# Low parts at three stage heads: subtracted by VectorE instead of GpSimd

## The chip, the cores and the metric

The kernel runs on one core of a Trainium2 chip. The metric is device time in microseconds (us), from the first to the last instruction and what lies around them, of one execution of the whole program. Engines are called as in the profile: PE (matrix products) with PEld (its weight loads), DVE (VectorE), ACT (ScalarE), POOL (GpSimd), SP (SyncE, which here only starts transfers).

## What is computed

A decoder trunk of two layers on 256 tokens of width 1024, in float32. Each layer has a token mixer and a channel mixer, and after each of the four the sum with the input is normalised.

```python
x = layernorm(ALPHA * x + mixer_ab(x))      # gated linear attention | top-k sparse attention
x = layernorm(ALPHA * x + swiglu(x))        # dense, 1024 -> 2816 -> 1024
x = layernorm(ALPHA * x + mixer_cd(x))      # forgetting attention | dilated attention
x = layernorm(ALPHA * x + moe(x))           # the best 2 of 8 experts, 1024 -> 3584 -> 1024
def swiglu(x, w1, w3, w2): return (silu(x @ w1) * (x @ w3)) @ w2
```

The router takes x @ w_router, keeps the two best experts of a token and weighs their outputs by a softmax of the two values.

## The kernel before, in words

**Products in three parts.** Every large product is made in a shorter float format of PE (float32r), with each operand split in a high part (the value cast to float32r) and a low part (value minus high part). `mm3` (lines 190 to 195) sums high x high, low x high and high x low in one PSUM bank. So each weight has to be split on its way from memory to PE, and so has each activation.

**Weights.** `piece` (from line 142) loads one piece of a weight, mostly 1 MB, in a raw buffer of a ring (`raw`), and splits it in two or four cuts: ACT casts the high part `whi` (line 165), and another engine subtracts it to get the low part `wlo` (line 167). There are six buffers of each, and the ring has 5 raw buffers at first and 13 at the end. The transfers are started on SP (line 152) and wait there, in order, until a raw buffer is free, that is until its last subtraction is done. Normally the subtraction is DVE's. A counter, `pool_lo`, gives the next one, two or three pieces to POOL instead:

```python
        eng = nc.vector
        if self.pool_lo > 0:
            self.pool_lo -= 1
            eng = nc.gpsimd
```

It is set to 2 ahead of the first pieces of the dense network (line 710) and of the second mixer (line 738), and to 1 ahead of the experts (line 955). The pieces there are, for the dense network, the two halves of the first 512 columns of w1 (four cuts of 1024 columns); for the second mixer, a piece of 264 columns (four cuts of 528) and one of 256 columns (two cuts of 1024); for the experts the first half of the first expert's w1 (two cuts of 1024).

**A stage's head.** A stage ends with a residual norm in two token tiles of 128 tokens. For each tile DVE adds the product to x (line 258, two steps), makes the mean (274), subtracts it and multiplies by the gain (279, two steps), makes the variance (281); ACT squares (276) and POOL takes the reciprocal root (282); DVE finishes x (285, two steps). Then PE transposes x (238), ACT casts the high part xTh (187) and DVE subtracts the low part xTl (188), each in two halves per tile. The first products of the next stage need xTh, xTl, whi and wlo. They are made for the first token tile while the second is still in its norm.

**The experts' head.** `begin`, in `moe_fast`, is written out by hand for PE, ACT, DVE and POOL. The router's values of a tile go through lines 845 to 848 (`best_two`), then a cast of the indices to float (857), a compare (859) and a sum to `sel` (861). PE counts the tokens in front (865, 866), DVE makes `slot` (867) and one-hot matrices `G` (908), and PE gathers the tokens of an expert by products of G with the high parts `xh` and the low parts `xl` of x (913). ACT and DVE take the results out of PSUM (919, 921). The split of x in xh and xl is line 964 (ACT) and 965 (POOL).

**Order.** Outside the hand-written part, a scheduler that simulates the program sets the order of the instructions of each engine. Each engine works in that order and waits at its instruction until the operands are there.

Of the kernel before, what the change touches and what calls it, by code (L numbers as in the profile page):

```python
# [9 lines left out]
F32 = mybir.dt.float32  # L10
# [66 lines left out]
def drain(*gens):  # L77
    for g in gens:
        for _ in g:
            pass  # L80
# [23 lines left out]
def lead(n, k):  # L104

    return [(t, i) for i in range(n - k) for t in range(NT)] + [(t, i) for t in range(NT) for i in range(n - k, n)]


class Trunk:
    def __init__(self, ctx, tc, io):  # L110
        self.ctx, self.tc, self.nc, self.io = ctx, tc, tc.nc, io
        self.pool_lo = 0
        pool = lambda name, bufs, **kw: ctx.enter_context(tc.tile_pool(name=name, bufs=bufs, **kw))
        self.cst = pool("cst", 1)
        self.raw = pool("raw", 5)
        self.rings, self.turn = [self.raw] * 5, 0
        self.hip = pool("hip", 6)
        self.lop = pool("lop", 6)
        self.dram = pool("dram", 1, space=DRAM)
        self.junk = dict(tag="X", bufs=2)  # L120
        self.ps = pool("ps", 4, space=PSUM)
        self.pa = pool("pa", 4, space=PSUM)
# [19 lines left out]
    def piece(self, src, later=False, cuts=2, raw=None):  # L142

        nc = self.nc
        srcs = src if isinstance(src, list) else [src]
        n, w = srcs[0].shape[1], sum(s.shape[2] for s in srcs)
        raw = (self.ring(n * w) if raw is None else raw).rearrange("p (n w) -> p n w", n=n)
        c = 0  # L150
        for s in srcs:
            nc.sync.dma_start(raw[:, :, c:c + s.shape[2]], s)
            c += s.shape[2]
        eng = nc.vector
        if self.pool_lo > 0:
            self.pool_lo -= 1
            eng = nc.gpsimd
        h = n // cuts
        parts = {}

        def split(i):
            sl = slice(i * h, (i + 1) * h)
            hi = self.hip.tile([128, h, w], F32R, name="whi", tag="whi")
            lo = self.lop.tile([128, h, w], F32R, name="wlo", tag="wlo")
            nc.scalar.copy(hi, raw[:, sl])  # L165
            parts[i] = hi, lo
            return lambda: eng.tensor_sub(lo, raw[:, sl], hi.bitcast(F32))  # L167

        part = lambda j, c0, c1: [a[:, j % h, c0:c1] for a in parts[j // h]]
        if later:  # L170
            return part, split
        for i in range(cuts):
            split(i)()
        return part
# [509 lines left out]
    def ffn(self, x):  # L684
        nc, io = self.nc, self.io
        with ExitStack() as st:
            pool = lambda n, b: st.enter_context(self.tc.tile_pool(name=n, bufs=b))
            acts, early = pool("acts", 2), pool("early", 1)
            self.wk, m = pool("wk1", 1), pool("m1", 1)
            xT = self.pair(early, [128, KT, S], "xT")  # L690
            gT = [m.tile([128, DFF // 128, S], F32R, name=n) for n in ("gTh", "gTl")]
            for c0 in range(0, DFF, 512):
                wd = min(512, DFF - c0)
                act = acts.tile([128, NT, 512], F32, name="act")

                def e1(t, p):
                    nc.scalar.activation(act[:, t, :wd], p, AF.Silu)

                def e3(t, p):
                    nc.vector.tensor_mul(act[:, t, :wd], act[:, t, :wd], p)  # L700
                    q = self.abank()
                    for j in range(wd // 128):
                        nc.tensor.transpose(q[:, j * 128:(j + 1) * 128], act[:, t, j * 128:(j + 1) * 128],
                                            self.ident)
                    sl = (slice(None), slice(c0 // 128, (c0 + wd) // 128), slice(t * 128, (t + 1) * 128))
                    self.split(gT[0][sl], gT[1][sl], q[:, :wd].rearrange("p (a b) -> p a b", b=128))

                first = self.proj_n(io["w1_dense"], c0, wd, xT, e1)
                if c0 == 0:
                    self.pool_lo = 2  # L710
                    self.transposed(xT, x, 0)
                    drain(islice(first, 2))
                    self.transposed(xT, x, 1)
                drain(first, self.proj_n(io["w3_dense"], c0, wd, xT, e3))
            drain(self.out_proj(io["w2_dense"], lambda k: [a[:, k] for a in gT], lead(DFF // 256, 3), x, 0, 1))


    def mixer_cd(self, x, scr, spare):
        nc, io = self.nc, self.io
        w = io["w_in_cd"]  # L720
        with ExitStack() as st:
# [13 lines left out]
                nc.scalar.copy(vc[:, t, 256:512], p[:, 0:256])  # L735
                nc.vector.tensor_copy(fz[:, t], p[:, 256:264])

            self.pool_lo = 2
            self.turn = 5
            first = [self.proj_n(w, 1280, 264, xT, evac_f), self.proj_n(w, 1024, 256, xT, self.evac_n(vc))]  # L740
            for t in range(NT):
# [158 lines left out]
    def moe_fast(self, x):  # L900

        nc, io, f, late = self.nc, self.io, self.f, self.late
# [3 lines left out]
        def one_hot(G, e, t):  # L906
            for a in range(2):
                nc.vector.tensor_scalar(G[:, t, a], self.iota[:, 1:129], self.slot[:, t, e + a:e + a + 1],
                                        None, op0=OP.is_equal)

        def collect(p, G, i, k, t):
            for j in range(2):
                nc.tensor.matmul(p[:, j * 256:(j + 1) * 256], self.xhl[i][:, t, (k + j) * 128:(k + j + 1) * 128],
                                 G[:, t], start=(t == 0 and j == 0), stop=(t == 1), skip_group_check=True)
# [8 lines left out]
        def xg_tiles():  # L923
            return [[self.xg.tile([128, KT, 128], F32R, name=n, bufs=2) for n in ("xgh", "xgl")] for a in range(2)]
# [24 lines left out]
        def begin():  # L949

            xh, xl = self.xhl
            E = mybir.EngineType
            G = f.tile([128, NT, 2, 128], F32R, name="G")
            xg = xg_tiles()
            self.pool_lo = 1
            part, split = [], []
            for w, k0 in (("w1_moe", 0), ("w1_moe", 4), ("w3_moe", 0)):
                p, sp = self.piece(self.rows(io[w][0], k0, 4, 0, 512), later=True)
                part.append(p)
                split.append(sp)  # L960
            ph = [self.abank() for _ in range(KT // 2)]

            def parts(t):
                nc.scalar.copy(xh[:, t], x[:, t])
                nc.gpsimd.tensor_sub(xl[:, t], x[:, t], xh[:, t].bitcast(F32))

            with self.tc.manual_schedule(engines={E.PE, E.Activation, E.DVE, E.Pool}):
                pos = self.bank()
                parts(0)
                with self.tc.issue_after(self.squares.ins):  # L970
                    lo = [split[0](0), split[0](1)]
                with self.tc.issue_after(self.power.ins):
                    for l in lo:
                        l()
                self.logits(1)
                best = self.route(f, pos)
                parts(1)
                lo = [split[1](0), split[1](1)]
                for t in range(NT):
                    one_hot(G, 0, t)  # L980
                for k in range(0, KT, 2):
                    for t in range(NT):
                        collect(ph[k // 2], G, 0, k, t)
                for l in lo:
                    l()
                for a in range(2):
                    for k in range(0, KT, 2):
                        evacuate(xg, ph[k // 2], 0, k, a)
                for l in (split[2](0), split[2](1)):
                    l()  # L990
                self.combine_weights(*best)
            for k in range(0, KT, 2):
                p = self.abank()
                for t in range(NT):
                    collect(p, G, 1, k, t)
                for a in range(2):
                    evacuate(xg, p, 1, k, a)
            transposed_one_hot(G, 0, xg)
            q = self.abank()
            for t in range(NT):  # L1000
                nc.tensor.matmul(q[:, 0:8], self.ones, self.sel[:, t], start=(t == 0), stop=(t == 1))
            mx = f.tile([128, 1], F32, name="mx")
            nc.vector.tensor_reduce(mx, q[:, 0:8], axis=AX.X, op=OP.max)
            nc.vector.tensor_copy(self.mxi, mx)
            return part
# [59 lines left out]

        SP = (0, 2, True, 0)
        ahead = begin()
        prev = None
        for e, c in product(range(NE), range(NC)):
# [18 lines left out]
            if (e, c) == (0, 3):  # L1088
                x = self.xp.tile([128, NT, D], F32, name="sum", tag="x")
# [139 lines left out]
```

## Time and profile before

| | us |
|---|---|
| median of three runs | 1510.81 (1510.8 to 1512.51) |
| the profiled execution, its time | 1513.67 |
| its span, first to last instruction | 1511.8 |
| PE busy in the span | 1462.5 (97%) |
| DVE busy | 1201.2 (79%) |
| ACT busy | 1025.9 (68%) |
| POOL busy | 91.2 (6%) |
| `wlo` subtractions on DVE (799) | 953.8, mean 1.229 each |

The mean granted clock of PE is 0.981 of full speed. The stages lie in the span as follows: first mixer up to about 168 us, dense network to 363, second mixer to 497, experts to the end. A row of a timeline gives the start, the duration (of the whole group if several alike follow each other), the engine, the line, the operation, what it writes and reads, the shape, the count, and in brackets how long the engine stood idle ahead of it and what ended that. Matrix instructions overlap, so the distance between the starts of two tells more than their durations.

### The profile page before, as it was taken

Reading aid. Unit: us, or ns where it says so; the run is one execution under the profiler, and the core shown is the slowest. Engines: PE = TensorE matmul, PEld = TensorE weight load, DVE = VectorE, ACT = ScalarE, POOL = GpSimd, SP = SyncE. Lnnn points to the kernel's source line nnn. Section 1 sums busy time; section 2 is a strip of 40 time slices with the busy share of each in tenths; the row PEclk is TensorE's granted clock in tenths of the full one; section 3 lists DMA queues with packets and bytes.
Section 4 is the critical chain, followed back from the end, with each engine's and each line's share of the span. In section 5 each row is a group of like instructions: output and inputs, shape, how many; then the busy total and the mean of one; then the engine's idle time right before and its main releaser. Section 6 shows DMA issues by size and latency. Waiting matters only on the chain. (4 is left out here: it accounts for less than half of the span.)

```text
span 1511.8 us, 19538 instructions
## 1 busy us (share of the span) xinstructions
PE 1462.5 (97%) x7226; PEld 1208.5 (80%) x7226; DVE 1201.2 (79%) x1394; ACT 1025.9 (68%) x1328; POOL 91.2 (6%) x85
## 2 busy tenths in 40 slices
PE   6999899998999799999999999999999999999996
PEld 5987688887987688888888888888888887888885
DVE  3697464545555899999999999989889889889987
ACT  3647444433676678878878878887777677777764
POOL 2223300003100230000000000000000000000000
PEclk8999999999999899999999999999999999999998
DMA  8844465556546689999989999999999999999971
GB/s 218 256 139 130 169 232 194 176 187 197 179 121 242 206 298 388 392 355 367 373 319 370 371 363 362 375 327 351 374 335 354 359 358 324 378 358 359 364 259 57
DMA packets 199459, 435.99 MB, mean 288 GB/s; under 512 B 9298, under 2 KB 33658, under 8 KB 199360
## 3 DMA queue, kind: packets, MB, share of 16 engines
q1 hardware_dynamic: 195760, 429.88, 79.7%
q10 hardware_dynamic: 2848, 2.95, 1.1%
q0 software_dynamic: 752, 1.88, 0.5%
q8 instruction: 58, 0.95, 0.3%
q14 instruction: 41, 0.34, 0.1%
HBM read 432.77 MB, written 1.84 MB: 287 GB/s over the span
## 5 line engine op out<-in xcount | busy, mean ns | idle before, releaser
L167 DVE TENSOR_TENSOR wlo<-raw,whi 128x1024 fp32r<-128x1024 f32 (+1 forms) x799 | 953.8, 1229 | 157.7 <-ACT whi L165 137.5
L165 ACT CAST whi<-raw 128x1024 fp32r<-128x1024 f32 (+1 forms) x811 | 821.1, 1046 | 209.8 <-PE bank L195 133.0
L193 PE MATMUL bank<-whi,xgh 128*128 128x512 f32 x896 | 353.9, 396 | 0.0
L194 PE MATMUL bank<-wlo,xgh 128*128 128x512 f32 x896 | 352.4, 393 | 0.0
L195 PE MATMUL bank<-whi,xgl 128*128 128x512 f32 x896 | 351.0, 392 | 0.1
L194 PEld LDWEIGHTS bank<-wlo,xgh 128*128 128x128 f32 x896 | 168.5, 188 | 40.5 <-DVE wlo L167 4.8
L195 PEld LDWEIGHTS bank<-whi,xgl 128*128 128x128 f32 x896 | 168.3, 188 | 36.7 <-ACT xgl L919 0.4
L193 PEld LDWEIGHTS bank<-whi,xgh 128*128 128x128 f32 x896 | 168.5, 188 | 35.6
L194 PE MATMUL y<-wlo,gTh 128*128 128x512 f32 x440 | 173.5, 394 | 0.0
L195 PE MATMUL y<-whi,gTl 128*128 128x512 f32 x440 | 171.6, 392 | 0.7 <-DVE gTl L188 0.7
L193 PE MATMUL y<-whi,gTh 128*128 128x512 f32 x440 | 149.3, 392 | 0.0
L195 PE MATMUL bank<-whi,xTl 128*128 128x512 f32 (+2 forms) x288 | 108.3, 377 | 9.7 <-DVE xTl L188 9.7
L193 PE MATMUL bank<-whi,xTh 128*128 128x512 f32 (+2 forms) x288 | 107.8, 375 | 2.6 <-ACT xTh L187 2.6
L194 PE MATMUL bank<-wlo,xTh 128*128 128x512 f32 (+2 forms) x288 | 107.5, 374 | 0.0
L195 PEld LDWEIGHTS y<-whi,gTl 128*128 128x128 f32 x440 | 82.6, 188 | 18.4 <-DVE gTl L188 1.2
L194 PEld LDWEIGHTS y<-wlo,gTh 128*128 128x128 f32 x440 | 82.7, 188 | 17.8 <-DVE wlo L167 0.3
L193 PEld LDWEIGHTS y<-whi,gTh 128*128 128x128 f32 x440 | 82.6, 188 | 17.8
L187 ACT CAST gTh<-abank 128x512 fp32r<-128x512 f32 (+1 forms) x67 | 38.8, 579 | 73.8 <-PE y L194 53.8
L193 PE MATMUL bank<-xTh,whi 128*128 128x256 f32 (+1 forms) x264 | 78.9, 299 | 7.6 <-ACT whi L165 7.6
L282 POOL TENSOR_TENSOR lnst<-lnst,mhalf 128x1 f32<-128x1 f32 x8 | 4.9, 613 | 1235.3 <-DVE lnst L281 1235.3
L195 PE MATMUL bank<-xTh,wlo 128*128 128x256 f32 (+1 forms) x264 | 78.5, 300 | 0.7 <-DVE wlo L167 0.7
L194 PE MATMUL bank<-xTl,whi 128*128 128x256 f32 (+1 forms) x264 | 78.5, 298 | 0.0
(293 smaller groups left out, 1478.4 us busy)
## 6 DMA issues: line engine op xcount, KB each, us to landing
raw<-in_w_moe SPq DMA_DIRECT2D x333, 1024.0 KB, 6.7
raw<-in_w_dense SPq DMA_DIRECT2D x33, 1024.0 KB, 5.1
raw<-in_w_in_ab SPq DMA_DIRECT2D x13, 1024.0 KB, 11.8
raw<-in_w_in_cd SPq DMA_DIRECT2D x11, 1024.0 KB, 5.9
raw<-in_w_out_ab SPq DMA_DIRECT2D x4, 1024.0 KB, 5.0
raw<-in_w_out_cd SPq DMA_DIRECT2D x4, 1024.0 KB, 5.8
T<-scr_bias ACTq DMA_DIRECT2D x8, 256.0 KB, 5.4
raw<-in_w_moe SPq DMA_DIRECT2D x3, 512.0 KB, 4.2
```

What stands on the lines that cost most here:

```text
L165: nc.scalar.copy(hi, raw[:, sl])
L167: return lambda: eng.tensor_sub(lo, raw[:, sl], hi.bitcast(F32))
L187: self.nc.scalar.copy(hi, src)
L193: mm(out, a[0], b[0], start=start, stop=False, skip_group_check=True)
L194: mm(out, a[0], b[1], start=False, stop=False, skip_group_check=True)
L195: return mm(out, a[1], b[0], start=False, stop=stop, skip_group_check=True)
L282: self.power = nc.gpsimd.tensor_tensor(st[:, 5:6], st[:, 4:5], self.mhalf[:, 0:1], op=OP.pow)
```

## The change

The counter is gone, and with it POOL's subtractions: all of them are DVE's. In the experts' head, where the order is written by hand, the subtractions also move: they come behind the one-hot matrices and the gather of the high parts, the first weight subtraction first, then the two of x, then the other weight subtractions.

```diff
@@ piece @@
-        eng = nc.vector
-        if self.pool_lo > 0:
-            self.pool_lo -= 1
-            eng = nc.gpsimd
...
-            return lambda: eng.tensor_sub(lo, raw[:, sl], hi.bitcast(F32))
+            return lambda: nc.vector.tensor_sub(lo, raw[:, sl], hi.bitcast(F32))
@@ ffn, mixer_cd, begin @@
-                    self.pool_lo = 2
-            self.pool_lo = 2
-            self.pool_lo = 1
@@ begin @@
-            def parts(t):
-                nc.scalar.copy(xh[:, t], x[:, t])
-                nc.gpsimd.tensor_sub(xl[:, t], x[:, t], xh[:, t].bitcast(F32))
+            def low(t):
+                nc.vector.tensor_sub(xl[:, t], x[:, t], xh[:, t].bitcast(F32))
...
-                parts(0)
+                nc.scalar.copy(xh[:, 0], x[:, 0])
                 with self.tc.issue_after(self.squares.ins):
                     lo = [split[0](0), split[0](1)]
-                with self.tc.issue_after(self.power.ins):
-                    for l in lo:
-                        l()
                 self.logits(1)
                 best = self.route(f, pos)
-                parts(1)
-                lo = [split[1](0), split[1](1)]
+                nc.scalar.copy(xh[:, 1], x[:, 1])
+                lo += [split[1](0), split[1](1)]
...
-                for l in lo:
+                lo[0]()
+                low(0)
+                low(1)
+                for l in lo[1:]:
                     l()
```

Line numbers of the changed kernel are 5 to 9 lower from `piece` on (line 167 is 162 there, 188 is 183, 258 is 253, 274 is 269, 279 is 274, 908 is 901). POOL loses fourteen rows and DVE gains them; no instruction of PE, ACT or SP is added or taken away.

On DVE at the dense network's head (lnst are the norm's sums, lngb its gain and bias), from the second token tile's residual on, before:

```order
L258 SCALAR_TENSOR_TENSOR xcur,lnst<-xcur,bank 128x512 x2
L167 TENSOR_TENSOR wlo<-raw,whi 128x1024
L274 TENSOR_SCALAR lnst<-lnst 128x1
L167 TENSOR_TENSOR wlo<-raw,whi 128x1024
L188 TENSOR_TENSOR xTl<-abank,xTh 128x4x128
```

and now:

```order
L162 TENSOR_TENSOR wlo<-raw,whi 128x1024 x3
L253 SCALAR_TENSOR_TENSOR xcur,lnst<-xcur,bank 128x512
L162 TENSOR_TENSOR wlo<-raw,whi 128x1024
L253 SCALAR_TENSOR_TENSOR xcur,lnst<-xcur,bank 128x512
L162 TENSOR_TENSOR wlo<-raw,whi 128x1024 x2
L183 TENSOR_TENSOR xTl<-abank,xTh 128x4x128 x2
```

Six subtractions stand ahead of xTl where two stood, and the mean (line 274, now 269) has moved behind xTl.

On DVE at the second mixer's head, from the first token tile's variance on, before:

```order
L281 TENSOR_SCALAR lnst<-lnst 128x1
L285 SCALAR_TENSOR_TENSOR xcur<-bank,lnst,lngb 128x512 x2
L258 SCALAR_TENSOR_TENSOR xcur,lnst<-xcur,bank 128x512 x2
L274 TENSOR_SCALAR lnst<-lnst 128x1
L279 SCALAR_TENSOR_TENSOR bank<-xcur,lnst,lngb 128x512 x2
L188 TENSOR_TENSOR xTl<-abank,xTh 128x4x128 x2
```

and now:

```order
L162 TENSOR_TENSOR wlo<-raw,whi 128x528
L280 SCALAR_TENSOR_TENSOR xcur<-bank,lnst,lngb 128x512 x2
L162 TENSOR_TENSOR wlo<-raw,whi 128x528 x3
L253 SCALAR_TENSOR_TENSOR xcur,lnst<-xcur,bank 128x512 x2
L162 TENSOR_TENSOR wlo<-raw,whi 128x1024
L269 TENSOR_SCALAR lnst<-lnst 128x1
L162 TENSOR_TENSOR wlo<-raw,whi 128x1024
L183 TENSOR_TENSOR xTl<-abank,xTh 128x4x128
L274 SCALAR_TENSOR_TENSOR bank<-xcur,lnst,lngb 128x512 x2
L183 TENSOR_TENSOR xTl<-abank,xTh 128x4x128
```

The six subtractions are there now, and the first half of xTl has moved ahead of the two steps of line 279 (now 274).

On DVE at the experts' head, from the one-hot matrices G on, before:

```order
L908 TENSOR_SCALAR G<-iota,slot 128x128 x4
L167 TENSOR_TENSOR wlo<-raw,whi 128x1024 x4
L875 TENSOR_TENSOR f_4483<-comb 128x2
L921 CAST xgl<-abank 128x256 x4
```

and now:

```order
L901 TENSOR_SCALAR G<-iota,slot 128x128 x4
L162 TENSOR_TENSOR wlo<-raw,whi 128x1024
L956 TENSOR_TENSOR xl<-xcur,xh 128x1024 x2
L162 TENSOR_TENSOR wlo<-raw,whi 128x1024 x5
L868 TENSOR_TENSOR f_4480<-comb 128x2
L914 CAST xgl<-abank 128x256 x4
```

Two subtractions of x and two of weights have come in; all that stands ahead of G is as it was.

## Rows read from the trace of the kernel before

**Rows 1.** Page, part 1: busy us (share of span) and instructions of each engine

```profile
PE 1462.5 (97%) x7226; PEld 1208.5 (80%) x7226; DVE 1201.2 (79%) x1394; ACT 1025.9 (68%) x1328; POOL 91.2 (6%) x85
```

**Rows 2.** Table by stretches: us, busy (x) of PE, PEld, DVE, ACT, POOL, PEclk, DMA share, GB/s

```profile
184.00:354.00 170.00, 170.00 (x818) 142.84 (x817) 86.88 (x85) 73.68 (x83) 0.00 (x0) 1.00 0.63 205
...
565.00:800.00 235.00, 235.00 (x1069) 193.17 (x1068) 219.14 (x213) 187.21 (x205) 0.00 (x0) 1.00 0.99 365
```

**Rows 3.** Waits of SP's queue, 600 to 700 us: us in total, times, longest

```profile
SPq L152 <- DVE wlo L167: 85.8, 35, 4.5
```

**Rows 4.** Timeline of POOL: start, us, line, operation, out<-in, count, idle before

```profile
163.09 10.41 POOL L167 TENSOR_TENSOR wlo<-raw,whi 128x1024 fp32r<-128x1024 f32 x4
...
358.41 5.21 POOL L167 TENSOR_TENSOR wlo<-raw,whi 128x528 fp32r<-128x528 f32 x4
...
364.22 4.66 POOL L167 TENSOR_TENSOR wlo<-raw,whi 128x1024 fp32r<-128x1024 f32 x2
...
500.81 4.67 POOL L167 TENSOR_TENSOR wlo<-raw,whi 128x1024 fp32r<-128x1024 f32 x2
```

**Rows 5.** Timeline of DVE, 380 to 390 us

```profile
382.61 4.63 DVE L167 TENSOR_TENSOR wlo<-raw,whi 128x1024 fp32r<-128x1024 f32 x4 [1.37 <-ACT whi L165]
...
388.36 0.16 DVE L781 TENSOR_TENSOR fz<-fz,bf 128x8 f32<-128x8 f32 x1
```

**Rows 6.** Timeline of DVE, dense head

```profile
162.99 1.41 DVE L285 SCALAR_TENSOR_TENSOR xcur<-bank,lnst,lngb 128x512 f32<-128x512 f32 x2 [0.67 <-POOL lnst L282]
...
168.49 2.81 DVE L167 TENSOR_TENSOR wlo<-raw,whi 128x1024 fp32r<-128x1024 f32 x1
...
171.34 3.23 DVE L167 TENSOR_TENSOR wlo<-raw,whi 128x1024 fp32r<-128x1024 f32 x1
174.50 0.68 DVE L188 TENSOR_TENSOR xTl<-abank,xTh 128x512 fp32r<-128x512 f32 x1
```

**Rows 7.** Timeline of DVE, second mixer's head

```profile
356.26 1.42 DVE L279 SCALAR_TENSOR_TENSOR bank<-xcur,lnst,lngb 128x512 f32<-128x512 f32 x2
...
361.93 0.69 DVE L258 SCALAR_TENSOR_TENSOR xcur<-xcur,bank 128x512 f32<-128x512 f32 x1 [2.04 <-PE bank L195]
...
363.30 0.69 DVE L258 SCALAR_TENSOR_TENSOR xcur<-xcur,bank 128x512 f32<-128x512 f32 x1 [0.67 <-PE bank L195]
...
364.27 5.83 DVE L279 SCALAR_TENSOR_TENSOR bank<-xcur,lnst,lngb 128x512 f32<-128x512 f32 x2
```

**Rows 8.** Timeline of DVE, experts' head

```profile
497.57 2.46 DVE L279 SCALAR_TENSOR_TENSOR bank<-xcur,lnst,lnkc 128x512 f32<-128x512 f32 x2
...
503.71 1.80 DVE L857 CAST f<-i 128x4 f32<-128x4 uint32 x1
505.55 2.28 DVE L859 TENSOR_TENSOR o<-iota,f 128x32 f32<-128x32 f32 x1
...
509.79 0.87 DVE L908 TENSOR_SCALAR G<-iota,slot 128x128 fp32r<-128x128 f32 x4
```

**Rows 9.** Timeline of PE, dense head

```profile
175.23 0.80 PE L195 MATMUL bank<-whi,xTl 128*128 128x512 f32 x1 [4.79 <-DVE xTl L188]
```

**Rows 10.** Timeline of PE, second mixer's head

```profile
370.75 0.59 PE L195 MATMUL bank<-whi,xTl 128*128 128x264 f32 x1 [4.95 <-DVE xTl L188]
```

**Rows 11.** Timeline of PE, experts' head

```profile
508.09 0.59 PE L866 MATMUL bank<-sel,sq 128*128 128x8 f32 x2 [6.17 <-DVE sel L861]
...
510.51 3.75 PE L913 MATMUL abank<-G,xh 128*128 128x256 f32 x16 [0.97 <-PE bank L866]
```

**Rows 12.** Timeline of ACT, dense head

```profile
167.18 2.00 ACT L165 CAST whi<-raw 128x1024 fp32r<-128x1024 f32 x2 [0.80 <-PE bank L195]
```

**Rows 13.** Table by stretches, slices of 1 us (columns as in rows 2)

```profile
178.00:179.00 1.00, 1.00 (x6) 0.83 (x5) 1.00 (x2) 0.00 (x0) 0.00 (x0) 0.91 1.06 414
364.00:365.00 1.00, 0.13 (x2) 0.00 (x0) 0.94 (x2) 1.00 (x2) 0.97 (x2) 1.00 0.53 29
...
376.00:377.00 1.00, 1.00 (x9) 1.00 (x9) 0.33 (x2) 0.37 (x1) 0.00 (x0) 0.92 1.05 387
```

More of the change, by code (lines that the diff above doesn't have):

```diff
@@ L111, in __init__ @@
         self.ctx, self.tc, self.nc, self.io = ctx, tc, tc.nc, io
-        self.pool_lo = 0
         pool = lambda name, bufs, **kw: ctx.enter_context(tc.tile_pool(name=name, bufs=bufs, **kw))
```

## The prediction

> **What bounds the kernel now.** I read the views in this order. The page's busy shares [rows 1]: PE is busy 97% of the span, DVE 79%, POOL 6%. Taken alone, that says that POOL's work is of no account. The table by stretches corrects it [rows 2]: in the dense network (184 to 354 us) and in the experts (565 to 800, and in the same way nearly to the end) PE is busy in the whole stretch at a granted clock of 1.00. There no other engine can make the kernel faster, and whatever PE loses or gains ahead of such a stretch is carried to the end. SP waits there for DVE: 35 waits, 85.8 us in 100 us, all for a raw buffer that DVE's subtraction frees [rows 3]. So transfers stand ready and are not the bound. What is left is the three heads, where PE stands still.
>
> POOL's list of instructions [rows 4] puts its subtractions exactly there: four from 163.09 us (10.41 us), four narrow and two wide from 358.41 (5.21 and 4.66 us), two from 500.81 (4.67 us; one xl subtraction stands ahead of these and one behind). The same subtraction of 1024 columns costs DVE 4.63 us for four, 1.16 us each from start to start [rows 5]. And beside POOL, DVE is slow. At the first head its own two subtractions take 2.81 and 3.23 us instead of 1.16, and xTl waits behind them [rows 6]. At the second, the two steps of L279 take 5.83 us; the same line took 1.42 us before POOL began [rows 7]. At the third, L279 takes 2.46 us, a cast of four columns 1.80 and a compare of 32 columns 2.28 [rows 8]; a small step of this kind costs 0.16 [rows 5]. PE waits for just these: 4.79 us for xTl [rows 9], 4.95 us for xTl [rows 10], 6.17 us for sel [rows 11].
>
> **The change, part by part.** It takes twelve weight subtractions and two xl subtractions from POOL and puts them on DVE: eight wide pieces and two xl at 1.16 [rows 5], and four of 528 columns at 0.68 (by xTl's 512 columns [rows 6]), 14.3 us of DVE work. For this DVE is no longer slowed. No DMA is added; POOL keeps the reciprocal roots and its DMA issues.
>
> The rows show DVE busy 219 of 235 us in the experts, where it still keeps ahead of PE [rows 2], and at the heads with steps that are long only beside POOL. The Trainium skill (Perfetto Trace Analysis, Optimizing Scalar/DVE Operations) speaks against this change: where VectorE is saturated, work may well be moved off it, to GpSimd too. By that rule all 14.3 us would come on top, 1525.1 us; by the rows the sum is the one that follows.
>
> *Dense head.* By the order, DVE now does three subtractions, half the residual, one, the other half, two, and only then xTl. DVE is free at 164.40 (162.99 + 1.41) [rows 6]; 6 x 1.16 + 2 x 0.69 = 8.3, so xTl starts at 172.7 and is there at 173.4 with 0.68 more; the last cast that this needs ends at 169.18 [rows 12], so no cast delays it. PE went on at 175.23 [rows 9]: it starts 1.8 us sooner. But PE's clock is down: granted 0.50 until it rises in the slice 178 to 179 [rows 13], so 2.7 us of work ran at half speed and cost 1.4. If it rises at the same moment, half of the gain is lost (0.9); if after as much work, 1.8 stays; if it never falls, 3.2. I take 1.2, since the idle stretch is still some 3 us, near the old one. The norm of the second token tile ends on DVE some 4 us behind xTl, as before; PE has over 6 us of work on the first tile, so that is covered; without this cover it would cost those 4.
>
> *Second mixer's head.* The four narrow subtractions (2.7 us) fall into the time in which DVE waits for PE ahead of the two residual steps (2.04 and 0.67 us [rows 7]); the second residual step still starts at 363.30 [rows 7]. Behind it: 0.69, a subtraction 1.16, the mean 0.2, a subtraction 1.16, xTl 0.68: 367.2. L279 now stands behind the first half of xTl. PE went on at 370.75 [rows 10], so 3.5 us come back. In the old run the clock fell in that idle time and rose only in the slice 376 to 377 [rows 13]: 5.3 us at half speed, 2.7 lost. With 1.6 us of idle time instead of 4.95 it may stay up; then the second half of xTl, 2 us behind the first because of L279, takes back some 0.7. Bounds: 1.8 (half speed until the same moment) and 5.5; as much slow work as before gives 3.5. The new gap is nearer to the pause at 364 to 365, which left the clock at 1.00 [rows 13], than to the 4.95: I take 4.4. Late next is the transfer of the mixer's last weight pieces, which needs raw buffers that these subtractions free; they are freed about 2 us sooner, so I count nothing, and up to 3 us if a cast had to wait for one.
>
> *Experts' head.* L279 gets back 1.0 (2.46 to 1.42 [rows 7, 8]), the cast 1.6, the compare 2.1 (each to 0.2): sel is there 4.7 us sooner. The weight and xl subtractions come behind the one-hot tiles. From the start of those (509.79 [rows 8]), xl is complete after 0.9 + 3 x 1.16 = 4.4 us; PE gathers the high parts from 0.7 us on for 3.75 us [rows 11], so xl is there just as it is needed. Three more weight subtractions follow (3.5 us), in the time in which ACT evacuates the gathered tiles and PE gathers the low parts. So I take 4.7. Bounds: 2.6, if the clock rises no sooner than before and the low parts are gathered at half speed too (some 2 us); 5.4, if it is up and sel 0.4 us earlier still.
>
> Sum: 1.2 + 4.4 + 4.7 = **10.3 us**, bounds 5.3 to 14.1. The profiled execution took 1513.67 us, of which 1511.8 is its span; 1513.67 - 10.3 = 1503.4. It lies 2.9 us above the median of 1510.81, so against that median I expect **1500.5 us**. About 3 us (0.2%) is what a measurement of this kernel can tell from no change.
>
> **The rivals.**
> 1. *The clock eats it.* Every head's gain at its lower bound: 5.3 us, 1505.5. For it: rows 13, twice half speed behind an idle PE. The Trainium skill (TensorE: Matmul & The Clock Gate, What's actually happening) says that the point at which the clock rises varies from run to run; the two heads, 2.7 and 5.3 us of slow work, agree.
> 2. *The clock stays up* at all three heads: 14.1 us, 1496.7. Against it: the first gap stays long, and the third head keeps tiny matmuls and a wait.
> 3. *The transfers become the bound.* The raw buffer of the first expert piece is freed 5 us later than by POOL: 500.81 + 4.67 = 505.5 before [rows 4], now 509.79 - 4.7 + 0.9 + 4 x 1.16 = 510.6, while PE starts 4.7 us sooner. If loads then set the pace, the third head's gain goes: 1510.8 - 5.6 = 1505.2, at worst nearly all of it. Against it: rows 3.
> 4. *DVE's backlog, slower.* If DVE's long steps at the heads are its own and not POOL's doing, the six subtractions before xTl cost about 3.0 us each [rows 6], and xTl of the dense head is there at 164.4 + 6 x 3.0 + 2 x 0.69 + 0.68 = 184.5 instead of 175.2, 9.3 us later; the second head loses 2.3 for two wide subtractions, the third 3.5 for three. Then 1510.8 + 15.1 = 1525.9. It decides if a wide subtraction at a head costs over 2 us with POOL at rest: some twelve stand on the three paths, and 10.3/12 is 0.9 above 1.16. Against it: 1.16 in rows 5, and L285, which kept its 1.41 us beside POOL [rows 6]. The Trainium skill (SBUF — State Buffer, Who interferes with whom) says that a VectorE instruction with two SBUF inputs and a GpSimd instruction that reads SBUF block each other for the length of one instruction, and that one SBUF input beside PSUM is free of it. L285's row agrees; the 5.83 us of L279 are more than one POOL subtraction (4.66/2) and its own 1.42 make, so rule and row do not cover each other, and 0.05 stays with this rival.
> 5. *The change does not do what it says*: out, the order shows POOL without these rows.
>
> **How the numbers follow.** Forecast (gain 7 to 13 us) 0.66; rival 1 0.14; rival 2 0.08; rival 3 0.07; rival 4 0.05. The range goes from 1497.0 (nearly rival 2) to 1506.0 (rivals 1 and 3 in their likely form): it leaves out rival 4, the worst of rival 3 and half of rival 2. Faster by over 0.2%: all but rival 4 and the worst of rival 3, 0.90; within 0.2%: 0.05; slower: 0.05.
>
> **What would show it.** In the profile afterwards: POOL about 30 us less busy; L279 at 1.4 us per pair at all heads; PE's waits for xTl near 3 and 1.6 us, for sel near 2; DVE little busier in all (14.3 added, some 13 of stretching gone). It is wrong if PE's stretch in the experts holds waits that were not there, if a wide subtraction at a head takes 2 us, or if the heads get shorter and the end does not move.

## The result and the profile after

The changed kernel takes 1500.68 us (median of six runs, 1496.93 to 1501.16), the kernel before, run beside it, 1511.65. The ratio is 0.992 with a 95% interval of 0.9909 to 0.993: 10.6 to 13.8 us faster. The forecast was 1500.5. One run reported below, the slowest of e6 with 3722.5 us, stands far apart from the rest and does not count in e6's ratio. The page after, part 1, busy time and share of the span (before: [rows 1]):

```profile
span 1498.4 us, 19533 instructions
...
PE 1461.3 (98%) x7226; PEld 1206.4 (81%) x7226; DVE 1201.1 (80%) x1408; ACT 1025.9 (68%) x1328; POOL 63.2 (4%) x71
```

POOL is 28.0 us less busy, and DVE, which does that work now, is as busy as before (1201.2): what was added is what the stretched steps gave back.

For the stages I count from the first residual step of one norm (L258, now L253) to that of the next, in the two profiled executions. The first rows stand at 159.24, 354.67 and 490.00 us before and here after:

```profile
157.39 0.69 DVE L253 SCALAR_TENSOR_TENSOR xcur<-xcur,bank 128x512 f32<-128x512 f32 x1 [1.06 <-PE bank L190]
...
352.13 0.69 DVE L253 SCALAR_TENSOR_TENSOR xcur<-xcur,bank 128x512 f32<-128x512 f32 x1 [4.94 <-PE bank L190]
...
482.71 0.69 DVE L253 SCALAR_TENSOR_TENSOR xcur<-xcur,bank 128x512 f32<-128x512 f32 x1 [1.05 <-PE bank L190]
```

| stage, us | before | after | gain | forecast (bounds) |
|---|---|---|---|---|
| up to the first residual step | 159.24 | 157.39 | 1.85 | 0 |
| dense network with its head | 195.43 | 194.74 | 0.69 | 1.2 (0.9 to 3.2) |
| second mixer | 135.33 | 130.58 | 4.75 | 4.4 (1.8 to 5.5) |
| experts to the end | 1021.80 | 1015.69 | 6.11 | 4.7 (2.6 to 5.4) |

The 1.85 us lie ahead of every row that changed and are no part of it: this point came at 156.97 to 159.85 us in the other profiles, at 159.12 in one with the whole change in it (e12 below). The mean granted clock of the stretch up to it was 0.94 in the profile before and 0.97 in this one. The three heads give 11.55.

DVE's timeline after, at the three heads (columns as in [rows 6] to [rows 8]):

```profile
162.46 3.49 DVE L162 TENSOR_TENSOR wlo<-raw,whi 128x1024 fp32r<-128x1024 f32 x3
...
170.49 1.28 DVE L183 TENSOR_TENSOR xTl<-abank,xTh 128x512 fp32r<-128x512 f32 x2
...
363.75 0.68 DVE L183 TENSOR_TENSOR xTl<-abank,xTh 128x512 fp32r<-128x512 f32 x1
364.36 1.41 DVE L274 SCALAR_TENSOR_TENSOR bank<-xcur,lnst,lngb 128x512 f32<-128x512 f32 x2
...
490.29 1.42 DVE L274 SCALAR_TENSOR_TENSOR bank<-xcur,lnst,lnkc 128x512 f32<-128x512 f32 x2
...
495.05 0.17 DVE L850 CAST f<-i 128x4 f32<-128x4 uint32 x1
495.25 0.19 DVE L852 TENSOR_TENSOR o<-iota,f 128x32 f32<-128x32 f32 x1
...
499.33 2.35 DVE L956 TENSOR_TENSOR xl<-xcur,xh 128x1024 fp32r<-128x1024 f32 x2
```

Every stretched step is short: L279 (now L274) 1.41 instead of 5.83, the cast 0.17 instead of 1.80, the compare 0.19 instead of 2.28, a wide subtraction 1.16. PE's waits follow ([rows 9] to [rows 11] answer; xgh and xgl are the gathered high and low parts):

```profile
171.22 0.80 PE L190 MATMUL bank<-whi,xTl 128*128 128x512 f32 x1 [2.63 <-DVE xTl L183]
...
364.49 0.39 PE L190 MATMUL bank<-whi,xTl 128*128 128x264 f32 x1 [1.12 <-DVE xTl L183]
...
495.71 0.60 PE L859 MATMUL bank<-sel,sq 128*128 128x8 f32 x2 [1.99 <-DVE sel L854]
...
498.10 3.68 PE L906 MATMUL abank<-G,xh 128*128 128x256 f32 x16 [0.94 <-PE bank L859]
...
505.50 0.50 PE L190 MATMUL bank<-whi,xgl 128*128 128x512 f32 x1 [0.58 <-ACT xgl L912]
```

The clock did not follow so neatly. Slices of 1 us of the table by stretches (the number ahead of the last two is the granted clock, as in [rows 13]); the first of each pair is where it fell, the second where it rose:

```profile
170.00:171.00 1.00, 0.00 (x0) 0.00 (x0) 1.00 (x2) 0.00 (x0) 0.00 (x0) 0.74 1.05 410
177.00:178.00 1.00, 1.00 (x5) 0.84 (x4) 0.00 (x0) 0.00 (x0) 0.00 (x0) 0.85 1.03 391
365.00:366.00 1.00, 1.00 (x8) 1.00 (x7) 1.00 (x3) 0.00 (x0) 0.00 (x0) 0.52 0.75 94
368.00:369.00 1.00, 1.00 (x9) 1.00 (x9) 0.58 (x1) 0.00 (x0) 0.00 (x0) 0.78 1.05 385
494.00:495.00 1.00, 0.00 (x0) 0.00 (x0) 0.93 (x9) 0.90 (x1) 0.00 (x0) 0.87 0.11 16
501.00:502.00 1.00, 1.00 (x6) 0.81 (x5) 1.00 (x2) 0.56 (x2) 0.00 (x0) 0.72 0.06 16
```

All three heads still fall to the lower level (0.50 in the slices between). In the long stretch of the experts the two rows that told that PE is the bound have not moved: PE busy throughout at 1.00, and SP waiting for DVE between 600 and 700 us (84.8 us, [rows 3] had 85.8).

```profile
565.00:800.00 235.00, 235.00 (x1072) 193.42 (x1071) 219.02 (x213) 187.26 (x204) 0.00 (x0) 1.00 0.99 365
...
SPq L151 <- DVE wlo L162: 84.8, 35, 4.1
```

### The profile page after: what moved, and what is told of

Same layout as the page of the kernel before. It is cut to its first block, busy times and chain, and to the rows that moved or that the text cites. A ratio compares the mean times of both kernels' runs of the same rounds, so it can differ in the third digit from the quotient of the medians.

```text
span 1498.4 us, 19533 instructions
## 1 busy us (share of the span) xinstructions
PE 1461.3 (98%) x7226; PEld 1206.4 (81%) x7226; DVE 1201.1 (80%) x1408; ACT 1025.9 (68%) x1328; POOL 63.2 (4%) x71
## 5 line engine op out<-in xcount | busy, mean ns | idle before, releaser
L183 DVE TENSOR_TENSOR gTl<-abank,gTh 128x512 fp32r<-128x512 f32 (+1 forms) x67 | 45.4, 678 | 31.3 <-ACT gTh L182 31.3
```

The costliest lines, as they stand in the source:

```text
L183: self.nc.vector.tensor_sub(lo, src, hi.bitcast(F32))
```

## The experiments

**Each head alone (e1, e2, e3).** The kernel before with one of the three parts of the change.

```diff
@@ e1: ffn @@
-                    self.pool_lo = 2
@@ e2: mixer_cd @@
-            self.pool_lo = 2
@@ e3: begin, as in the change @@
-            self.pool_lo = 1
...
```

> The kernel before with POOL's subtractions given to DVE at the dense network's head alone. Theory (POOL's reading stretches DVE's steps at each head, and each head passes its own gain to the end): the stretch from the last residual of the first mixer to the last residual of the dense network gets 0.7 us shorter, as between the two profiles, and could get up to 3 us shorter if the clock of PE stays up; 1509 to 1511 us. Rival (the gain comes from POOL being idle in general or needs all three heads): no change at all, or a loss, since six subtractions now stand ahead of xTl.

> The kernel before with POOL's subtractions given to DVE at the second mixer's head alone. Theory: PE's wait for xTl falls from 4.95 to about 1.1 us there and nowhere else; 4 to 5 us faster than the kernel before, about 1507. Rival (POOL's own lateness, not DVE's stretching, sets the wait): the same gain, but L279 keeps its 5.8 us.

> The kernel before with the experts' head of the changed kernel. Theory: the steps of lines 279, 857 and 859 are short, PE's wait for sel falls from 6.2 to about 2 us; 5 to 6 us faster, about 1506, and the three kernels with one head changed add up to the changed kernel's 11 us. Rival (gains overlap, for instance in transfers): the three add up to clearly more or less than 11 us.

Measured: e1 1509.69 us, ratio 0.9985 (0.9976 to 0.9994); e2 1505.63, 0.9961 (0.9948 to 0.9975); e3 1506.80, 0.9965 (0.9952 to 0.9979). The three add up to 0.0089, the whole change is 0.008: within their intervals (some 0.001 to either side) the heads are independent. By stages of their profiles: e1's dense network 194.68 (0.75 less than before), e2's mixer 129.09 (6.2 less), e3's experts 1016.1 (5.7 less). L279 takes 1.41 us in e2, so the rival named for it fails. e2's mixer beats the changed kernel's by 1.5 us with the same order. PE waits the same 1.12 us for xTl there, but the clock never falls:

```profile
366.08 0.39 PE L195 MATMUL bank<-whi,xTl 128*128 128x264 f32 x1 [1.12 <-DVE xTl L188]
...
368.00:369.00 1.00, 1.00 (x11) 1.00 (x10) 0.25 (x2) 0.00 (x0) 0.56 (x1) 1.00 1.05 403
```

e2 is alone in this. In the changed kernel and in e4 to e7 and e9 to e12, which have this order too, the clock fell at this head and the stage took 130.56 to 130.62 us. e2 is also the only one of them with the old dense network ahead of the head, so it is not shown whether the execution or the kernel makes the difference.

**The later place, on POOL (e4).** The changed kernel, with two weight subtractions and both of x in the experts' head given back to POOL, but started only when `slot` is there.

```diff
+                gate = f.tile([128, NT, 8], F32, name="gate")
+                nc.gpsimd.tensor_copy(gate, self.slot)
@@ low @@
-                nc.vector.tensor_sub(xl[:, t], x[:, t], xh[:, t].bitcast(F32))
+                nc.gpsimd.tensor_sub(xl[:, t], x[:, t], xh[:, t].bitcast(F32))
...
```

> The changed kernel with only the experts' head on POOL: the first piece's two and the two xl subtractions are POOL's again, but at the changed kernel's place, behind the routing (a small copy of slot on POOL holds them back). It tells the order from the engine. Theory (what costs is that POOL reads while DVE makes sel): sel comes as early as in the changed kernel, PE's wait for it is 2 us; then four subtractions of 2.3 us on POOL, 9.3 us where DVE needed 4.6, bring xl 3 to 4 us later, so 2 to 4 us slower than the changed kernel, 1503 to 1505. Rival (the engine alone matters, POOL is too slow wherever it stands): all of the experts' gain of 5 to 6 us is lost, 1506 to 1507.

Measured: 1501.39 us, ratio 0.993 (0.9917 to 0.9944), about a microsecond more than the changed kernel and less than expected. The total misleads here, and the head has to be read by its rows. PE waits 1.98 us for sel, as in the changed kernel: what the routing gains is POOL's silence during it. Then the same fault returns at the next DVE steps; POOL's rows and DVE's, and PE's wait:

```profile
498.32 2.35 POOL L167 TENSOR_TENSOR wlo<-raw,whi 128x1024 fp32r<-128x1024 f32 x1
500.63 2.33 POOL L962 TENSOR_TENSOR xl<-xcur,xh 128x1024 fp32r<-128x1024 f32 x1
...
497.98 5.07 DVE L906 TENSOR_SCALAR G<-iota,slot 128x128 fp32r<-128x128 f32 x4
502.97 6.74 DVE L167 TENSOR_TENSOR wlo<-raw,whi 128x1024 fp32r<-128x1024 f32 x2
...
503.20 3.33 PE L911 MATMUL abank<-G,xh 128*128 128x256 f32 x14 [3.77 <-DVE G L906]
...
512.60 0.50 PE L195 MATMUL bank<-whi,xgl 128*128 128x512 f32 x1 [0.25 <-ACT xgl L917]
```

G takes 5.07 us instead of 0.88. The first product with the low parts starts 29.31 us after the stage's first row (483.29), where it is 22.79 in the changed kernel and 27.99 in the one before: the later place on POOL gives the whole gain of the head away again. The stage is only 1.3 us longer than the changed kernel's (1017.0) because the products behind the head follow each other faster: from that first product to the end e4 needs 987.7 us, the changed kernel 992.9 and the other profiles 993.0 to 994.2. PE's groups in a stretch of 500 us, of the changed kernel (600 to 1100) and of e4 (607 to 1107):

```profile
L188 PE MATMUL bank<-whi,xgh 128*128 128x512 f32 x459 | 182.5, 398 | 0.0
...
L193 PE MATMUL bank<-whi,xgh 128*128 128x512 f32 x464 | 183.0, 394 | 0.0
```

The kernel before has 458 there, e5 458, e9 459, e11 460. That is 5 us over the experts, in a stretch where POOL subtracts no more (its last one ends at 508.6). In the source only the small tile `gate` reaches so far, behind which other tiles may lie elsewhere in SBUF; the trace differs in more, since ACT's casts of weights wait 9.5 us for DVE's subtractions in these 500 us and 0.9 in the changed kernel. What is the cause was not tried and stays open.

**POOL put back beside the routing, without its work on the path (e5, e6).** The changed kernel with three subtractions (e5, POOL reads and writes) or seven memsets (e6, it only writes) of 1024 columns behind the last reciprocal root, into a tile that is overwritten later.

```diff
+                waste = xl[:, 1]
+                with self.tc.issue_after(self.power.ins):
+                    for _ in range(3):
+                        nc.gpsimd.tensor_sub(waste, xh[:, 0].bitcast(F32), xh[:, 0].bitcast(F32))
@@ e6 @@
+                    for _ in range(7):
+                        nc.gpsimd.memset(waste.bitcast(F32), 0.0)
```

> The changed kernel with three idle subtractions of 1024 columns on POOL behind the second reciprocal root of the experts' head (they read xh twice and write in xl's second tile, which DVE overwrites later). Nobody needs their result. Theory (POOL's reading blocks DVE's steps with operands in SBUF): the cast of line 850 and the compare of line 852 take about 2 us each again, PE's wait for sel goes from 2 back to about 6 us, and the kernel is 3.5 to 4.5 us slower than the changed one, about 1504.5. Rival (it was the order or POOL's lateness): no change, 1500 to 1501.

> The same place and about the same time on POOL, but seven memsets of 1024 columns, which read nothing. Theory in its narrow form (it is the read side that POOL and DVE share): the compare of line 852, with two inputs in SBUF, stays at 0.2 us; at most the cast of line 850 gets longer; 0 to 1.5 us slower than the changed kernel. Rival (any work of POOL in SBUF blocks DVE): as with the reading ones, 3.5 to 4.5 us slower.

Measured: e5 1504.01 us, ratio 0.994 (0.9927 to 0.9953); e6 1502.74, 0.9932 (0.992 to 0.9945). POOL's row and DVE's in e5:

```profile
492.97 5.84 POOL L966 TENSOR_TENSOR xl<-xh 128x1024 fp32r<-128x1024 f32 x3
...
492.94 1.95 DVE L839 SCALAR_TENSOR_TENSOR slot<-slot,lnst,rsum 128x8 f32<-128x8 f32 x1
494.81 1.40 DVE L280 SCALAR_TENSOR_TENSOR xcur<-bank,lnst,lnvc 128x512 f32<-128x512 f32 x2
...
496.21 0.20 DVE L838 SCALAR_TENSOR_TENSOR slot<-rsum,lnst,abank 128x8 f32<-128x8 f32 x1
...
497.38 1.46 DVE L850 CAST f<-i 128x4 f32<-128x4 uint32 x1
...
499.33 0.60 PE L859 MATMUL bank<-sel,sq 128*128 128x8 f32 x2 [5.19 <-DVE sel L854]
```

A step of 8 columns takes 1.95 us (0.22 without), the cast of four 1.46 (0.17); L280 and L838, which take an operand from PSUM (`bank`, `abank`), are untouched. sel is 3.2 us later and the stage 3.5 us longer (1019.2), with nothing else changed. So long steps come back with nothing but POOL's subtractions beside them. In e6:

```profile
493.16 7.04 POOL L966 MEMSET xl<- 128x1024 f32 x7
...
494.96 0.21 DVE L839 SCALAR_TENSOR_TENSOR slot<-slot,lnst,rsum 128x8 f32<-128x8 f32 x1
...
495.68 0.49 DVE L850 CAST f<-i 128x4 f32<-128x4 uint32 x1
...
498.36 1.99 DVE L901 TENSOR_SCALAR G<-iota,slot 128x128 fp32r<-128x128 f32 x4
```

Beside POOL's writes alone L839 is as short as ever, and so is the compare (L852, 0.19), but the cast and G are still held (0.49 and 1.99 instead of 0.17 and 0.88); the stage is 1.8 us longer (1017.5), somewhat more than the 1.5 expected at most; G had not been thought of. The Trainium skill (SBUF — State Buffer, Who interferes with whom) says that a VectorE step with two SBUF inputs contends with GpSimd's reads and not with its writes alone, and that cast and tensor_scalar can enter modes that take both ports; both runs agree, L839 by its 1.95 and 0.21, cast and G by what they lose in e6; that these two were in such a mode no run shows.

**xTl first, dense head (e7).** The changed kernel with the casts and subtractions of the second matrix's first piece queued behind the first token tile's xTh and xTl, so that four wide subtractions stand ahead of xTl and not six.

```diff
+                third = self.proj_n(io["w3_dense"], c0, wd, xT, e3)
...
+                    drain(first)
+                    with self.tc.issue_after(cast.ins), self.tc.issue_after(rest.ins):
+                        next(third)
+                drain(first, third)
```

> The changed kernel with the dense network's head reordered: the casts and subtractions of w3's first pieces come behind the first token tile's xTh and xTl. Theory (PE waits 2.6 us for xTl because two subtractions that are not needed yet stand ahead of it, and this wait halves PE's clock for the next 6.5 us): PE's wait shrinks to under 0.5 us, the clock stays up, 3 to 5 us faster than the changed kernel, 1496 to 1498. Rival (the clock falls whatever the wait, or another chain sets the restart): 0 to 2 us faster.

Measured: 1496.53 us, ratio 0.9893 (0.9879 to 0.9907), 4.2 us below e8, its neighbour in the same series, whose dense head is the changed kernel's. PE waits 1.00 us instead of 2.63, and now the clock stays up; at 176.01 it waits 0.51 us for the second token tile's norm, the cover of which is used up:

```profile
170.21 0.50 PE L190 MATMUL bank<-whi,xTl 128*128 128x512 f32 x1 [1.00 <-DVE xTl L183]
...
176.01 1.31 PE L233 MATMUL abank<-sq,xcur 128*128 128x128 f32 x8 [0.51 <-DVE xcur L280]
...
174.00:175.00 1.00, 1.00 (x6) 0.84 (x5) 0.53 (x2) 0.58 (x1) 0.39 (x1) 1.00 0.69 82
```

The dense network takes 190.38 us, 4.4 less than in the changed kernel. PE goes on 2.3 us sooner (11.57 us after the first row instead of 13.83), by 1.6 of this wait and 0.6 of that for xTh; half of the 6.1 us that the changed kernel works at half speed (171.22 to 177.3) is 3.0; less the new 0.5, that makes 4.8, close to what came.

**xTl first, second mixer (e8).** The same edit at the mixer's head, for the second piece.

```diff
...
+                    drain(islice(first[0], 2))
+                    with self.tc.issue_after(cast.ins), self.tc.issue_after(rest.ins):
+                        next(first[1])
...
```

> The changed kernel with the second mixer's head reordered: both wide subtractions come behind both halves of xTl. Theory: PE's wait for xTl of 1.1 us goes and with it the half clock that followed (3.4 us of it, 1.7 lost); 1.5 to 3 us faster than the changed kernel, 1497.5 to 1499. Rival (the low part of the second piece is then late): PE waits for wlo instead, no change.

Measured: 1500.73 us, ratio 0.9918 (0.9905 to 0.993), as the changed kernel. The two subtractions are gone from ahead of xTl, but the scheduler put the norm's two steps there, and PE now waits for a weight's cast instead:

```profile
362.90 1.42 DVE L274 SCALAR_TENSOR_TENSOR bank<-xcur,lnst,lngb 128x512 f32<-128x512 f32 x2
...
364.23 1.28 DVE L183 TENSOR_TENSOR xTl<-abank,xTh 128x512 fp32r<-128x512 f32 x2
...
364.43 0.38 PE L188 MATMUL bank<-whi,xTh 128*128 128x256 f32 x1 [0.93 <-ACT whi L160]
```

The clock fell in the slice 365 to 366 all the same. The stage is 0.6 us shorter (130.01), which the runs cannot tell.

**Low parts gathered first, experts (e9).** The third weight piece queued behind the gather and evacuation of the low parts.

```diff
+                for k in range(0, KT, 2):
+                    p = self.abank()
+                    for t in range(NT):
+                        collect(p, G, 1, k, t)
+                    for a in range(2):
+                        evacuate(xg, p, 1, k, a)
                 for l in (split[2](0), split[2](1)):
                     l()
...
```

> The changed kernel, with the casts and subtractions of the third weight piece of the experts (line 160 and 162 in the head) queued behind the evacuation of the low parts (xgl). In the changed kernel PE waits 0.27 us for xgh and 0.58 us for xgl, and two casts of 1.0 us each stand on ACT between the two evacuations. Theory A (these waits are on the path): PE's wait for xgl goes, the time falls by 0.3 to 0.9 us. Theory B (the piece that now comes later is late in its turn, a wait for wlo or whi appears in PE's stretch): no gain, or 0.5 to 2 us slower.

Measured: 1500.51 us, ratio 0.9914 (0.9895 to 0.9934). PE's wait for xgl is gone from the trace, but the stage is no shorter (1016.0), and the time is not told apart from the changed kernel's. The first product with xgl starts 21.82 us after the first row instead of 22.79, but the rest takes 994.2 us instead of 992.9. Where the gain went back was not found; it is too small for these runs.

**PE kept busy in the experts' head (e10, e11).** Ten products that nothing uses, in PE's waits for sel and G; e11 has e7's edit too.

```diff
+            def idle(n):
+                for _ in range(n):
+                    nc.tensor.matmul(ph[0], xh[:, 0, 0:128], xh[:, 0, 512:1024], start=True, stop=True)
...
                 self.logits(1)
+                idle(7)
                 best = self.route(f, pos)
+                idle(3)
```

> The changed kernel with ten more products of 128x128 by 128x512 on PE in the experts' head, whose results are overwritten and used by nothing: seven behind the router's logits, where PE waits 1.99 us for sel, and three behind the sums of sel, where it waits 0.94 us for G. Theory A (the half clock in the head is the price of PE's idle time and of its tiny products there, and costs half of the 5.7 us of slow work): the granted clock stays at 1.00 or rises sooner, the 16 products of the gather take 2.2 instead of 3.7 us, the three sums 0.3 us each instead of 0.57, and the time falls by 1.5 to 2.8 us. Theory B (the clock falls all the same): each product takes 0.43 us, the seven end some 1 us behind sel and the three 0.4 us behind G, and the time rises by 0.5 to 1.5 us.

> Both edits together: the dense head's order with xTl ahead of the second matrix's subtractions (4.2 us below the changed kernel by itself) and the ten products in the experts' head. If the two places are independent, and the ten products help by 1.5 to 2.8 us, the time is 4.2 + 2 = 6 us below the changed kernel, about 1494.5 us (ratio 0.988 to the kernel before). If the ten products do not help, it is at 1496.5 to 1498.

Measured: e10 1501.56 us, ratio 0.9915 (0.9896 to 0.9933); e11 1498.03, 0.989 (0.987 to 0.991). Both theories came true, one in each profile. In e10 the clock fell in the slice 496 to 497:

```profile
495.58 2.80 PE L960 MATMUL abank<-xh 128*128 128x512 f32 x7
...
500.74 3.08 PE L906 MATMUL abank<-G,xh 128*128 128x256 f32 x16
...
496.00:497.00 1.00, 1.00 (x5) 0.76 (x4) 0.93 (x9) 0.90 (x1) 0.00 (x0) 0.60 0.20 29
```

In e11 it stayed at 1.00 throughout:

```profile
490.77 1.86 PE L965 MATMUL abank<-xh 128*128 128x512 f32 x7
...
494.78 2.39 PE L911 MATMUL abank<-G,xh 128*128 128x256 f32 x16
```

The stage takes 1015.9 us in e10, no better than without the products, and 1014.1 in e11. The price of the low clock in this head is thus some 2 us, by one profile each; the same products went with it in one and not in the other, and over the runs no gain is seen (e11 beside e7: 0.989 and 0.9893).

**Both orders (e12).** e7 and e9 together.

```diff
@@ ffn, as in e7 @@
+                third = self.proj_n(io["w3_dense"], c0, wd, xT, e3)
...
@@ begin, as in e9 @@
+                    for a in range(2):
+                        evacuate(xg, p, 1, k, a)
...
```

> The two orders together, without added products: xTl ahead of the second matrix's subtractions in the dense head (which brought 4.2 us by itself), and the low parts' evacuation ahead of the third weight piece in the experts' head (which took away PE's 0.58 us wait for xgl). If they are independent: the dense network takes 190.4 us from the first residual step to the next stage's first, with PE waiting 1.0 us for xTl and no slice below 1.00 there, and the time is 4.2 to 5.0 us below the changed kernel (a ratio of 0.989 to the kernel before). If the clock in the dense head falls in this execution all the same, the network takes 192 to 195 us and 2 to 4 us of it are lost again.

Measured: 1496.46 us, ratio 0.9895 (0.9878 to 0.9911), with a dense network of 190.37. That is e7's time: e7 is the version that beats both kernels, and no other edit adds to it measurably.

## Why the prediction was right, and where its terms were off

**The mechanism.** That POOL's subtractions stretch DVE's steps held at every head, and e5 shows it by itself. The rows named in advance came: POOL 28 us less busy (about 30), the norm's pair at 1.41 and 1.42, PE's waits 2.63, 1.12 and 1.99 (near 3, 1.6 and 2). The sum came closer than its terms: the dense head lies below its bounds and the experts above theirs, and the two misses partly cancel.

**Dense head: 1.2 forecast, 0.7 in the profile.** PE goes on 13.83 us after the stage's first row instead of 15.99, 2.2 sooner (forecast 1.8). The step that failed in this profile is "If it rises at the same moment, half of the gain is lost (0.9)", my lower bound: the clock rose later, counted from that row at 19.9 us instead of 18.9. So 6.1 us ran at half speed instead of 3.0, and 1.6 of the 2.2 went back. The other profiles with this order fall in two groups. In e1, e5 and e9 the clock rose 19.70 to 19.88 us after the first row, and the network took 194.65 to 194.71 us; in e4, e6, e8 and e10 it rose at 18.85 to 19.05, about as early as before, and the network took 194.26 to 194.35. With the old order (before, e2, e3) it took 195.39 to 195.55. So the head gave 0.7 to 0.8 us or 1.1 to 1.2, by where the clock rose, and the term of 1.2 was met in half of the profiles. e1's ratio gives 2.3 us (0.9 to 3.6), too wide to choose between the two. e7 shows what the head is worth when the clock stays up: 4 us more.

**Second mixer: 4.4 forecast, 4.75.** PE goes on 3.7 us sooner (12.36 after the first row instead of 16.08; forecast 3.5), and 1.0 is clock: 3.4 us at half speed instead of 5.4. I had thought it likelier that the clock stays up. Here it fell, so that the 4.4, a value between two cases, came so close is in part luck. It stayed up in e2, and the head gave 6.2 there, above my bound of 5.5: the 0.7 that the second half of xTl was to take back never came, since PE does not wait for it.

**Experts: 4.7 forecast, 6.1, above the bound of 5.4.** sel's sums start 13.00 us after the first row instead of 18.09, that is 5.1 sooner: the 4.7 of the sum and 0.4 of one more stretched step that the sum did not count. The row before and after:

```profile
502.55 0.64 DVE L846 SCALAR_TENSOR_TENSOR slot<-slot,lnst,rsum 128x8 f32<-128x8 f32 x1
...
494.33 0.21 DVE L839 SCALAR_TENSOR_TENSOR slot<-slot,lnst,rsum 128x8 f32<-128x8 f32 x1
```

The first product that needs the low parts starts 22.79 us after the first row instead of 27.99: 5.2 are still there, so xl, which I had just in time, cost nothing. The last 0.9 lie in the 993 us behind, where e1 and e2, with this head as before, are 0.5 and 0.8 us shorter than before too; I take them for the spread of executions. The clock rose 18.9 us after the first row instead of 26.1; I had put it at the old moment or at the start, and 5.9 us behind sel's sums ran at half speed instead of 8.0. That alone would be some 1 us more; the new waits of PE for the evacuated tiles, 0.27 us for xgh and 0.58 for xgl, took most of it back.

**The rivals.** Rival 1, the clock eats the gains, came at the dense head alone; the two heads that it names stand in one execution and could not show a spread from run to run. Rival 2 came in e2, e7 and e11, one head each of those it names. Rival 3: from 505 us to the end PE waits 1.6 us in all for evacuations and splits of activations, none of it for a transfer; its weight loads wait 4.5 us for wlo, before 4.8. Rival 4 is refuted by the wide subtractions at the heads, 1.16 us, and by e5; its sum was also too low, since by its own condition the five subtractions at the other two heads cost 3.0 us each and not 1.16 (9.3 + 6.0 + 9.0, 1535.1 us). The 1525.1 us, with all of POOL's work on top, did not come: DVE's busy time is unchanged at 1201 us. The Trainium skill (Perfetto Trace Analysis, Optimizing Scalar/DVE Operations), in the passage that the prediction puts beside that sum, adds that GpSimd and DVE share a read port, so that moving work between these two might not help; that half agrees.

## What to carry to other kernels

Ask what an engine does to its neighbours before counting its share: 28 us on an engine that was busy 6% cost 11, since short steps on the path stood beside them. A step of four columns that takes 1.5 us is the sign of it, and moving the work to a later place on the same engine only moved the stretched steps (e4). And a wait on PE has two prices: its own length, and half of the work that then runs at the lower clock; the second can be the larger and varies between profiles of one order, so a bound should let the clock rise later than before too.

## What was not expected of the hardware

One DVE step can wait for two subtractions of POOL that stand back to back, and not for one. In the kernel before, the first step of L279 at the second head is 5.17 us long, beside POOL's pair of 4.66 from 364.22 [rows 4]; the second took the remaining 0.66 of the pair's 5.83:

```profile
364.27 5.17 DVE L279 SCALAR_TENSOR_TENSOR bank<-xcur,lnst,lngb 128x512 f32<-128x512 f32 x1
```

So what the prediction left unexplained, a pair longer than one subtraction and its own time, fits the same blocking, won twice in a row by POOL. It is not always so: in e5 L839 waited for the first of three subtractions alone (1.95 us). The faster products of e4 are the second surprise. The third is how freely the clock differs. The Trainium skill (TensorE: Matmul & The Clock Gate, What's actually happening) says that the point at which the clock rises varies from run to run; the eight profiles with one order at the dense head agree, with a rise 18.85 to 19.91 us after the first row. Whether it falls at all differs too, in e2 against the changed kernel and in e10 against e11, each time in two kernels that are not the same elsewhere. But runs of one kernel differ as well: three of e10's six have a mean granted clock of 0.987 and take 1502.34 to 1504.04 us, the other three 0.990 to 0.993 and 1498.56 to 1500.77. At which place they differ, and what decides it, was not found.
